# Within a column of weight tiles: long and short matmuls in groups of two, or one after the other

## The chip, the core and the metric

The kernel runs on one core of one Trainium2 chip, as one program launched once. The metric is the device time of that program in microseconds (us); lower is better. Each kernel is timed several times and the median is given. A core has a matmul engine (TensorE, PE in the profile, whose weight loads the profile lists apart as PEld), a vector engine (VectorE, DVE), a scalar engine (ScalarE, ACT), GpSimd (POOL) and SyncE (SP), which here issues the weight transfers.

## The reference, cut to what matters

```python
for l in range(DEPTH):                                   # DEPTH = 2, SEQ = 256, D_MODEL = 2048
    h = _rmsnorm(x, norm1_g[l])
    p = (h @ w_in[l]).astype(f32)                        # 2048 -> 6144
    q, k, v, g, xb, yb = jnp.split(p, ...)
    o_ret = _retention(q, k, v, g, ...)                  # 8 heads
    o_lru = _rg_lru_branch(xb, yb, ...)                  # 1024 channels
    mix = jnp.concatenate([o_ret, o_lru], axis=-1)
    x = x + mix @ w_out[l]                               # 2048 -> 2048
    h = _rmsnorm(x, norm2_g[l])
    x = x + (silu(h @ ffn_w_gate[l]) * (h @ ffn_w_up[l])) @ ffn_w_down[l]   # 2048 -> 5632 -> 2048
return _rmsnorm(x, final_g)
```

Everything is float32. Nearly all of the work is in the matrix products with `w_in`, `w_out`, `ffn_w_gate`, `ffn_w_up` and `ffn_w_down`, for 256 tokens.

## The kernel before

**Float32 in three products.** A float32 number is split in two parts that the matmul engine takes in its one-pass format fp32r: hi is the number rounded to that format, lo is what is left. A product is then hi·hi + hi·lo + lo·hi. For weights, `split` (line 560 on) makes hi with a ScalarE copy (L568) and lo with a VectorE subtraction (L569), in two halves of a unit's weights. For activations, `pair` makes one tile `op` of 2 x 256 columns, hi beside lo.

**A column unit.** The weights of one block of 128 output channels are one unit, up to 16 tiles of 128 x 128. `column_unit` (L182) runs it: for each tile k, a long matmul (L195) with the weights' hi part moves the whole `op` tile, 512 columns, and a short one (L198) with the weights' lo part moves its hi half, 256 columns, into the right half of the same PSUM bank. All matmuls of a unit add into one bank `acc_ps` of 512 columns. When the unit is done the two halves are added by ScalarE and VectorE (L178, L179) or added to the residual (L406, L407). Below, H is a long matmul (L195) and L a short one (L198), each with its own load of 128 x 128 weights, and a pair is the H and the L of one tile.

**The order.** A unit is issued in blocks of four tiles. In each block the kernel takes two tiles at a time (L193): H, H, L, L, then the next two tiles the same way. A unit of 16 tiles is eight such groups; one of 14 tiles seven; one of 15 tiles seven and a last tile alone, H, L.

There are 384 column units in the two layers: 80 of `w_in` (16 tiles), 32 of `w_out` (16), 176 of gate and up (16), 64 of `w_down` with 15 tiles and 32 with 14. That is 80·16 + 32·16 + 176·16 + 64·15 + 32·14 = 6016 tiles. The columns of `w_in` that give v are computed by other code (`v_units`, L441 to L443), where three long matmuls of 512 columns follow one another in turn; the change does not touch them.

**What runs beside it.** The weights of unit n + 2 are split in two halves while unit n runs (at its blocks 0 and 2), and the transfer of unit n + 3 is issued then. There are three buffers each of raw weights, hi and lo, and four PSUM banks for units. A list of ticks places the small work of the heads (scores, decays, normalization) between blocks; their small matmuls, of tile `sm_ps`, stand between blocks on PE. The engines' queues are laid down when the program is built, by a scheduler that may move an instruction past neighbours it does not depend on.

Of the kernel before, what the change touches and what calls it, by code (L numbers as in the profile page):

```python
# [80 lines left out]
def trunk(ctx: ExitStack, tc, a, out):  # L81
# [100 lines left out]
    def column_unit(src, n_k, operand, done, begin=None, order=None):  # L182

        u = Unit(src, n_k * P, [], begin=begin)
        order = order or list(range(n_k))

        def block(i):
            ks = order[i : i + 4]

            def run():  # L190
                if i == 0:
                    u.ps = big_ps.tile([P, 512], F32, tag="big", name="acc_ps")
                for pr in (ks[:2], ks[2:]):  # L193
                    for k in pr:
                        PE.matmul(u.ps, lhsT=u.hi[:, k * P : (k + 1) * P],  # L195
                                  rhs=operand(k).rearrange("p a t -> p (a t)"), start=k == order[0], stop=False)
                    for k in pr:
                        PE.matmul(u.ps[:, T : 2 * T], lhsT=u.lo[:, k * P : (k + 1) * P], rhs=operand(k)[:, 0, :],  # L198
                                  start=False, stop=k == order[-1])
            return run  # L200

        u.blocks += [block(i) for i in range(0, n_k, 4)]
        u.done = lambda: done(u.ps)
        return u
# [542 lines left out]
```

## Time and profile before

| | |
|---|---|
| median of 3 runs | 2257.88 us (2257.45 to 2258.04) |
| the profiled execution | 2257.48 us |
| its span, first to last instruction | 2255.7 us |
| PE busy | 2239.1 us (99%) |
| PEld busy | 1949.4 us (86%) |
| DVE busy | 1512.5 us (67%) |
| ACT busy | 1127.1 us (50%) |
| granted TensorE clock, mean | 0.998 |

The span is the profiled execution without what lies around it, 1.8 us here. Busy time of PE is the union of its matmuls' records; the records overlap, since a matmul's record runs on while the next has begun. How fast the matmuls follow one another is therefore read from their starts, not from their durations. A row of the timeline merges instructions of one line that follow one another, and gives the start of the first.

### The profile page before, as it was taken

The numbers are of one execution on the slowest core, as the hardware profiler recorded it, in microseconds if no ns is written. First come the engines' busy times: TensorE is split into PE (matmuls) and PEld (weight loads), VectorE is DVE, ScalarE is ACT, GpSimd is POOL, SyncE is SP. The second block draws the span as 40 slices with busy tenths as digits, with TensorE's granted clock in tenths as the row PEclk, the third lists the DMA queues.
The fourth block names the chain that finished last, engine by engine and source line by source line (L and its number), as shares of the span: only waits on it lengthen the run. The fifth ranks groups of instructions, "written<-read, shape, count | busy, mean of one in ns | idle before, by whom it ended". The sixth has DMA issues, their size and how long they took to land.

```text
span 2255.7 us, 31764 instructions
## 1 busy us (share of the span) xinstructions
PE 2239.1 (99%) x12760; PEld 1949.4 (86%) x12760; DVE 1512.5 (67%) x2405; ACT 1127.1 (50%) x1648; POOL 59.8 (3%) x97
## 2 busy tenths in 40 slices
PE   9999999999999999999999999999999999999997
PEld 7888888888888888888888888888888888888886
DVE  6888876666566655666748889766665666556665
ACT  6667544544344443444546665444443444334453
POOL 0010100000000000000000101000000000000000
PEclk9999999999999999999999999999999999999999
DMA  7555555555555555555555554555555555555553
GB/s 286 183 186 181 172 195 191 183 191 189 184 200 187 186 186 189 188 190 179 201 193 179 180 197 165 189 182 192 191 183 195 188 187 184 192 188 190 193 175 112
DMA packets 63140, 422.92 MB, mean 187 GB/s; under 512 B 7312, under 2 KB 7952, under 8 KB 24592
## 3 DMA queue, kind: packets, MB, share of 16 engines
q1 hardware_dynamic: 60912, 414.60, 52.5%
q0 software_dynamic: 1792, 5.24, 0.8%
q8 instruction: 100, 1.64, 0.3%
q10 hardware_dynamic: 288, 1.05, 0.1%
q14 instruction: 48, 0.39, 0.0%
HBM read 418.77 MB, written 2.10 MB: 187 GB/s over the span
## 4 chain that ended last, share of the span: by engine, by line
PE 97%; DVE 1%; issue 0%; DMA 0%; POOL 0%; ACT 0%; SPq 0%; DVEq 0%; POOLq 0%
PE acc_ps L195 62%; PE acc_ps L198 31%; PE v_ps L442 1%; PE v_ps L443 1%; PE v_ps L441 1%; PE sm_ps L331 1%; DVE wlo L569 0%; PE sm_ps L240 0%; DMA raw<-in_w_v_dram 0%; DVE op L130 0%; PE sm_ps L289 0%; PE sm_ps L157 0%; PE sm_ps L241 0%; PE sm_ps L256 0%; PE sm_ps L255 0%
## 5 line engine op out<-in xcount | busy, mean ns | idle before, releaser
L195 PE MATMUL acc_ps<-op,whi 128*128 128x512 f32 x6016 | 1899.8, 397 | 0.0
L198 PEld LDWEIGHTS acc_ps<-op,wlo 128*128 128x128 f32 x6016 | 1129.8, 188 | 263.4
L569 DVE TENSOR_TENSOR wlo<-raw,whi 128x1024 fp32r<-128x1024 f32 (+3 forms) x808 | 950.0, 1187 | 366.6 <-ACT whi L568 362.4
L198 PE MATMUL acc_ps<-op,wlo 128*128 128x256 f32 x6016 | 1188.6, 278 | 0.0
L568 ACT ACTIVATE whi<-raw 128x1024 fp32r<-128x1024 f32 (+3 forms) x808 | 817.3, 1029 | 657.3 <-PE acc_ps L195 578.1
L195 PEld LDWEIGHTS acc_ps<-op,whi 128*128 128x128 f32 x6016 | 920.4, 189 | 4.8 <-DVE op L127 0.7
L406 DVE TENSOR_TENSOR x<-acc_ps,x 128x256 f32<-128x256 f32 x128 | 54.2, 424 | 215.5 <-PE acc_ps L198 215.5
L126 ACT ACTIVATE op<-mix 128x256 fp32r<-128x256 f32 x104 | 43.1, 416 | 167.7 <-DVE mix L510 163.5
L505 ACT ACTIVATE sg<-z 128x256 f32<-128x256 f32 x88 | 36.8, 419 | 161.1 <-DVE z L504 161.1
L179 DVE TENSOR_TENSOR z<-acc_ps,low 128x256 f32<-128x256 f32 x256 | 106.7, 417 | 0.0
L178 ACT ACTIVATE low<-acc_ps 128x256 f32<-128x256 f32 x256 | 93.7, 366 | 0.0
L127 DVE TENSOR_TENSOR op<-mix,op 128x256 fp32r<-128x256 f32 x104 | 44.0, 424 | 42.7 <-ACT op L126 42.6
L509 DVE TENSOR_TENSOR sg<-sg,rs 128x256 f32<-128x256 f32 x88 | 37.4, 425 | 42.6 <-ACT sg L505 42.6
L407 DVE TENSOR_TENSOR x<-acc_ps,x 128x256 f32<-128x256 f32 x128 | 54.2, 424 | 4.3
L150 POOL TENSOR_TENSOR rc<-rc,mhalf 128x2 f32<-128x2 f32 x7 | 5.8, 824 | 1720.7 <-DVE rc L149 1720.7
L442 PE MATMUL v_ps<-wlo,op 128*128 128x512 f32 x128 | 50.1, 391 | 1.1 <-DVE wlo L569 1.1
L441 PE MATMUL v_ps<-whi,op 128*128 128x512 f32 x128 | 50.1, 396 | 0.5 <-ACT op L129 0.4
L443 PE MATMUL v_ps<-whi,op 128*128 128x512 f32 x128 | 50.1, 391 | 0.0
L510 DVE TENSOR_TENSOR mix<-z,sg 128x256 f32<-128x256 f32 x88 | 36.7, 417 | 0.0
L504 DVE TENSOR_TENSOR z<-z,rs 128x256 f32<-128x256 f32 x88 | 36.7, 417 | 0.0
L129 ACT ACTIVATE op<-x,par 128x256 fp32r<-128x256 f32 x64 | 31.2, 496 | 2.6 <-DMA par<-in_par_dram 1.8
L173 DVE TENSOR_TENSOR acc<-acc,sq 128x256 f32<-128x256 f32 x73 | 30.6, 420 | 1.6 <-ACT sq L172 1.0
(116 smaller groups left out, 698.9 us busy)
## 6 DMA issues: line engine op xcount, KB each, us to landing
raw<-in_w_gate_dram SPq DMA_DIRECT2D x88, 1024.0 KB, 4.8
raw<-in_w_up_dram SPq DMA_DIRECT2D x88, 1024.0 KB, 4.8
raw<-in_w_in_dram SPq DMA_DIRECT2D x80, 1024.0 KB, 4.8
raw<-in_w_down_dram SPq DMA_DIRECT2D x64, 960.0 KB, 4.7
raw<-in_w_out_dram SPq DMA_DIRECT2D x32, 1024.0 KB, 4.8
raw<-in_w_down_dram SPq DMA_DIRECT2D x32, 896.0 KB, 4.6
raw<-in_w_v_dram SPq DMA_DIRECT2D x12, 1024.0 KB, 4.8
raw<-in_w_v_dram SPq DMA_DIRECT2D x16, 256.0 KB, 6.0
```

The costliest lines, as they stand in the source:

```text
L127: V.tensor_tensor(out=t[:, 1, :], in0=x_ap, in1=t[:, 0, :].bitcast(F32), op=ALU.subtract)
L178: S.activation(out=low, in_=ps[:, T : 2 * T], func=AF.Copy)
L179: V.tensor_tensor(out=z, in0=ps[:, 0:T], in1=low, op=ALU.add)
L195: PE.matmul(u.ps, lhsT=u.hi[:, k * P : (k + 1) * P], rhs=operand(k).rearrange("p a t -> p (a t)"), start=k == order[0], stop=False)
L198: PE.matmul(u.ps[:, T : 2 * T], lhsT=u.lo[:, k * P : (k + 1) * P], rhs=operand(k)[:, 0, :], start=False, stop=k == order[-1])
L406: V.tensor_tensor(out=X[:, k, :], in0=ps[:, T : 2 * T], in1=X[:, k, :], op=ALU.add)
L407: V.tensor_tensor(out=X[:, k, :], in0=ps[:, 0:T], in1=X[:, k, :], op=ALU.add)
L441: PE.matmul(ps, lhsT=x2[:, 0, t], rhs=u.hi[:, w], start=k == 0, stop=False)
L442: PE.matmul(ps, lhsT=x2[:, 0, t], rhs=u.lo[:, w], start=False, stop=False)
L443: PE.matmul(ps, lhsT=x2[:, 1, t], rhs=u.hi[:, w], start=False, stop=k == KD - 1)
L568: S.activation(out=u.hi[:, w], in_=u.raw[:, w], func=AF.Copy)
L569: V.tensor_tensor(out=u.lo[:, w], in0=u.raw[:, w], in1=u.hi[:, w].bitcast(F32), op=ALU.subtract)
```

## The change

One line of `column_unit` changes.

```diff
                 if i == 0:
                     u.ps = big_ps.tile([P, 512], F32, tag="big", name="acc_ps")
-                for pr in (ks[:2], ks[2:]):
+                for pr in (ks[:2], ks[2:3], ks[3:]) if i == 0 else [[k] for k in ks]:
                     for k in pr:
                         PE.matmul(u.ps, lhsT=u.hi[:, k * P : (k + 1) * P],
                                   rhs=operand(k).rearrange("p a t -> p (a t)"), start=k == order[0], stop=False)
```

The first two tiles of a unit keep H, H, L, L. Every other tile is taken alone: its H, then its L. No instruction is added or removed, and the operands of each are the same.

On PE, here are the first matmuls of one `w_in` unit of the first layer (`acc_ps` is its bank, `op` the tile k's activations, `whi` and `wlo` the unit's weights), in the kernel before:

```order
L195 MATMUL acc_ps_2101<-op_142,whi_1956 128x512
L195 MATMUL acc_ps_2101<-op_147,whi_1956 128x512
L198 MATMUL acc_ps_2101<-op_142,wlo_1957 128x256
L198 MATMUL acc_ps_2101<-op_147,wlo_1957 128x256
L195 MATMUL acc_ps_2101<-op_152,whi_1956 128x512
L195 MATMUL acc_ps_2101<-op_162,whi_1956 128x512
L198 MATMUL acc_ps_2101<-op_152,wlo_1957 128x256
L198 MATMUL acc_ps_2101<-op_162,wlo_1957 128x256
L195 MATMUL acc_ps_2101<-op_169,whi_1956 128x512
L195 MATMUL acc_ps_2101<-op_182,whi_1956 128x512
L198 MATMUL acc_ps_2101<-op_169,wlo_1957 128x256
L198 MATMUL acc_ps_2101<-op_182,wlo_1957 128x256
```

and in the changed kernel:

```order
L195 MATMUL acc_ps_2101<-op_142,whi_1956 128x512
L195 MATMUL acc_ps_2101<-op_147,whi_1956 128x512
L198 MATMUL acc_ps_2101<-op_142,wlo_1957 128x256
L198 MATMUL acc_ps_2101<-op_147,wlo_1957 128x256
L195 MATMUL acc_ps_2101<-op_152,whi_1956 128x512
L198 MATMUL acc_ps_2101<-op_152,wlo_1957 128x256
L195 MATMUL acc_ps_2101<-op_162,whi_1956 128x512
L198 MATMUL acc_ps_2101<-op_162,wlo_1957 128x256
L195 MATMUL acc_ps_2101<-op_169,whi_1956 128x512
L198 MATMUL acc_ps_2101<-op_169,wlo_1957 128x256
L195 MATMUL acc_ps_2101<-op_182,whi_1956 128x512
L198 MATMUL acc_ps_2101<-op_182,wlo_1957 128x256
```

From the third tile on, the second H of a group and the first L have changed places. The last L of a group stands where it stood, so a unit begins and ends with the same kinds of matmul.

The scheduler also moves a few neighbours on the other engines. On VectorE, in the last third of `w_down` (14 tiles a unit; L569 makes lo of the weights, L173 and L130 belong to the norm that follows), before:

```order
L406 TENSOR_TENSOR x<-acc_ps,x 128x256
L407 TENSOR_TENSOR x<-acc_ps,x 128x256
L569 TENSOR_TENSOR wlo<-raw,whi 128x896
L173 TENSOR_TENSOR acc<-acc,sq 128x256
L569 TENSOR_TENSOR wlo<-raw,whi 128x896
L130 SCALAR_TENSOR_TENSOR op<-x,par,op 128x256
```

and in the changed kernel:

```order
L406 TENSOR_TENSOR x<-acc_ps,x 128x256
L407 TENSOR_TENSOR x<-acc_ps,x 128x256
L569 TENSOR_TENSOR wlo<-raw,whi 128x896 x2
L173 TENSOR_TENSOR acc<-acc,sq 128x256
L130 SCALAR_TENSOR_TENSOR op<-x,par,op 128x256
```

The second half of the split now stands ahead of the norm's addition. At six other places in the two layers a neighbour on VectorE or ScalarE has moved by one or two instructions in the same way; GpSimd and SyncE are as before.

## Rows read from the trace of the kernel before

**Rows 1.** The page: span, busy time of engines, granted clock, chain that ended last.

```profile
span 2255.7 us, 31764 instructions
...
PE 2239.1 (99%) x12760; PEld 1949.4 (86%) x12760; DVE 1512.5 (67%) x2405; ACT 1127.1 (50%) x1648; POOL 59.8 (3%) x97
...
PEclk9999999999999999999999999999999999999999
...
PE acc_ps L195 62%; PE acc_ps L198 31%; PE v_ps L442 1%; PE v_ps L443 1%; PE v_ps L441 1%; PE sm_ps L331 1%; DVE wlo L569 0%; PE sm_ps L240 0%; DMA raw<-in_w_v_dram 0%; DVE op L130 0%; PE sm_ps L289 0%; PE sm_ps L157 0%; PE sm_ps L241 0%; PE sm_ps L256 0%; PE sm_ps L255 0%
```

**Rows 2.** Waits of PE alone: who, for whom: us in total, times, longest us.

```profile
PE sm_ps L289 <- DVE on L275: 2.1, 2, 1.0
PE sm_ps L666 <- DVE sq L538: 1.4, 1, 1.4
PE v_ps L442 <- DVE wlo L569: 1.1, 2, 0.6
PE sm_ps L614 <- DVE sp L584: 1.0, 1, 1.0
PE sm_ps L157 <- POOL rc L150: 1.0, 1, 1.0
PE v_ps L441 <- ACT op L129: 0.4, 2, 0.2
```

**Rows 3.** Timeline, PE, gate and up units: start us, us, engine, line, op.

```profile
400.81 0.63 PE L195 MATMUL acc_ps<-op,whi 128*128 128x512 f32 x2
401.28 0.39 PE L198 MATMUL acc_ps<-op,wlo 128*128 128x256 f32 x2
401.51 0.62 PE L195 MATMUL acc_ps<-op,whi 128*128 128x512 f32 x2
...
551.29 0.63 PE L195 MATMUL acc_ps<-op,whi 128*128 128x512 f32 x2
```

**Rows 4.** Timeline, PE, units of 14 tiles.

```profile
1057.81 0.63 PE L195 MATMUL acc_ps<-op,whi 128*128 128x512 f32 x2
...
1116.33 0.63 PE L195 MATMUL acc_ps<-op,whi 128*128 128x512 f32 x2
```

**Rows 5.** Timeline, PE, units of 15 tiles: the last tile alone, the next unit.

```profile
577.58 0.40 PE L195 MATMUL acc_ps<-op,whi 128*128 128x512 f32 x1
577.81 0.28 PE L198 MATMUL acc_ps<-op,wlo 128*128 128x256 f32 x1
577.92 0.62 PE L195 MATMUL acc_ps<-op,whi 128*128 128x512 f32 x2
...
578.62 0.63 PE L195 MATMUL acc_ps<-op,whi 128*128 128x512 f32 x2
...
635.48 0.64 PE L195 MATMUL acc_ps<-op,whi 128*128 128x512 f32 x2
635.96 0.40 PE L198 MATMUL acc_ps<-op,wlo 128*128 128x256 f32 x2
636.20 0.62 PE L195 MATMUL acc_ps<-op,whi 128*128 128x512 f32 x2
...
640.73 0.62 PE L195 MATMUL acc_ps<-op,whi 128*128 128x512 f32 x2
```

**Rows 6.** Timeline, PE, units of v: long matmuls only.

```profile
1133.89 0.39 PE L441 MATMUL v_ps<-whi,op 128*128 128x512 f32 x1
1134.12 0.39 PE L442 MATMUL v_ps<-wlo,op 128*128 128x512 f32 x1
...
1170.39 0.39 PE L443 MATMUL v_ps<-whi,op 128*128 128x512 f32 x1
```

**Rows 7.** Timeline, PE and PEld, one group: weight loads beside the matmuls.

```profile
1000.95 0.39 PE L198 MATMUL acc_ps<-op,wlo 128*128 128x256 f32 x2
1000.95 0.19 PEld L198 LDWEIGHTS acc_ps<-op,wlo 128*128 128x128 f32 x1
1001.06 0.30 PEld L195 LDWEIGHTS acc_ps<-op,whi 128*128 128x128 f32 x2
1001.17 0.63 PE L195 MATMUL acc_ps<-op,whi 128*128 128x512 f32 x2
```

**Rows 8.** Timeline, PE and DVE: a unit's start, the split in it, two units later.

```profile
1014.41 0.40 PE L195 MATMUL acc_ps<-op,whi 128*128 128x512 f32 x1
1015.52 1.22 DVE L569 TENSOR_TENSOR wlo<-raw,whi 128x1024 fp32r<-128x1024 f32 x1 [1.64 <-ACT whi L568]
...
1017.00 1.21 DVE L569 TENSOR_TENSOR wlo<-raw,whi 128x1024 fp32r<-128x1024 f32 x1
...
1025.56 0.40 PE L195 MATMUL acc_ps<-op,whi 128*128 128x512 f32 x1
```

## The prediction

> **What bounds the kernel now.** I read the page first: PE is busy 99% of the span, and 93% of the chain that ended last is L195 and L198 [rows 1]. The waits come next: PE waits for another engine some 7 us in all [rows 2], and none of these waits is of a column unit. The granted clock is at nine tenths or more in all 40 slices, with a mean of 0.998, so TensorE stands at the upper of its two levels, 2.4 GHz [rows 1]. The kernel is therefore a stream of matmuls that follow one another at PE's own pace, and the change permutes that stream. Nothing but the pace can answer to it, so the pace is what the rest of the reading is about.
>
> The pace is read from starts. From 400.81 to 551.29 lie 27 gate and up units without a break, 27 x 16 = 432 pairs of H and L: 150.48 / 432 = 348.3 ns a pair, or 696.7 ns a group H, H, L, L [rows 3]. From 1057.81 to 1116.33 lie 12 units of 14 tiles, 168 pairs: 58.52 / 168 = 348.3 ns again [rows 4]. The border between two units thus costs nothing, and the group is all there is to explain. Inside one group the starts read 400.81, 401.28, 401.51: the two H's take 0.47 us and the two L's 0.23 [rows 3].
>
> **The change part by part.** *What moves.* Each unit keeps its first group. Of the 6016 tiles that leaves 6016 - 2 x 384 = 5248, of which 64 (the last of a 15-tile unit) stood alone already. So 5184 tiles, in 2592 groups, go from H, H, L, L to H, L, H, L. No instruction, byte or flop comes or goes. The sum is 5184 times the difference between a pair in the new order and 348.3 ns: each nanosecond is 5.2 us, 0.23% of the kernel. That is the whole difficulty, and 0.2% (4.5 us) is also about what a measurement of this kernel can tell from no change.
>
> *The fixed part of a matmul.* Another stream in the same trace has long matmuls only. The v units run from 1133.89 to 1170.39 in 161 steps, 36.50 / 161 = 226.7 ns a matmul of 512 columns [rows 6]. If 512 columns at 2.4 GHz take 213.3 ns, one by clock, what is left is 13.4 ns a matmul. A group has four matmuls and 2 x 512 + 2 x 256 = 1536 columns: 640.0 + 4 x 13.4 = 693.6 ns. Measured are 696.7, so some 3.1 ns of a group are not explained by the number of matmuls and columns. Order can act on these, and their size is that of the disputed term: 2592 x 3.1 = 8.0 us. A group has one change from long to short and one back, one H after H and one L after L. If the 3.1 ns belong to the changes of length, the new order has them in every pair, and 8.0 us are added. If they belong to the repeats, L after L above all, the new order has none, and 8.0 us go. Neither row decides it by itself; the resolution of the starts (0.01 us over 161 steps, 0.06 ns) is not the problem.
>
> *What a lone pair costs.* The one place where the trace already shows the new order is the last tile of a 15-tile unit: L, L, H, L, H, H [rows 5]. From 577.92 to 640.73 lie 12 such units, 62.81 us; at 348.3 ns a pair the 180 pairs would take 62.70. So each of these units is 0.11 / 12 = 9 ns longer than its number of pairs asks, and since borders are free [rows 4], that is the price of setting one lone H, L into a stream of groups. The pair itself is nearly the usual length, 577.58 to 577.92, 0.34 to 0.35 us. The rest comes behind it: the first group of the next unit takes 0.70 us in one unit (577.92 to 578.62) and 0.72 in another (635.48 to 636.20), and these two kinds alternate [rows 5]. A lone pair is never shown to gain anything, which speaks for the changes of length as what costs, not the repeats. I take +8.0 us for the pairs from this.
>
> *The way back at the head of each unit.* The changed kernel returns to H, H, L, L in every unit's first group, as the 15-tile units do now. Of the 9 ns 1.6 are in the term above (3.1 / 2); 7.4 remain. The 64 units of 15 tiles pay it already: (384 - 64) x 7.4 = 2.4 us. Its bounds are 0 and 9 ns, 0 to 2.9 us.
>
> *Weight loads.* Each matmul has its load, which starts as the matmul ahead of it starts: the load of the second L is at 1000.95, when the first L starts, and that of the next H at 1001.06, 0.11 before 1001.17 [rows 7]. The next load therefore lies beside the current matmul, and a short one leaves about 0.11 us for it. In both orders two loads of each group lie beside a long matmul and two beside a short one, so the count asks for nothing. Whether two tight loads in a row (before) or one tight and one easy in turn (after) is the better is the question of the 3.1 ns again.
>
> The Trainium skill ("TensorE: Matmul & The Clock Gate", sections "Back-to-back issue gap" and "Step-by-step: what each phase is for") says that the next weights are loaded into a background buffer while a matmul streams, and that warm matmuls follow one another at columns / 2.4 + 2.5 ns. An estimate from it is 215.8 + 109.2 = 325.0 ns a pair in either order, so the change would be worth nothing. The trace does not agree on the amount (348.3 ns [rows 3]), so something beside columns and that floor is paid here, and the page does not say whether it asks for an order; that the order is free is the first rival below.
>
> *Waits, buffers and the other engines.* The last H of a unit now ends one L later ahead of the unit's end, about 0.12 us nearer to it, and it frees that unit's hi buffer; the split that takes the buffer is of a later unit. In the unit that starts at 1014.41 the two halves of lo are made at 1015.52 and 1017.00, and PE reads them two units later, from 1025.56 on [rows 8]. The cover is 7 us or more against 0.12 us. In the last third of w_down the second half of the split is moved ahead of the norm's addition on VectorE, which moves each by about one instruction, some 1.2 us at most by the length of a split [rows 8]; VectorE is busy 67% of the span [rows 1] and nothing on PE waits for it there [rows 2]. Without that cover each such delay would be 0.1 to 1.2 us in a unit. I count 0, with 0 to 1 us in all as the range. The small matmuls stand between blocks as before.
>
> The sum: 8.0 + 2.4 = +10.4 us. Against the profiled execution, 2257.48 us (span 2255.7 and 1.8 around it), this gives 2267.9; that execution lies 0.4 below the median of the runs, so the median after should be about 2268.3.
>
> **The rivals.**
>
> *The order is free.* Each matmul costs its columns and a fixed part wherever it stands, and the 3.1 ns are something that any mixture of lengths pays. Then only the way back is left: 2257.9 + 2.4 = 2260.3 us, +0.1%. For it: v's fixed part explains 693.6 of 696.7 ns. Against it: the 9 ns of a lone pair show that the order acts.
>
> *The repeats were the cost* (faster). L after L puts two loads in a row under matmuls that leave 0.11 us each [rows 7]; a long matmul between them gives the loads time again. Its place is the second L of each group, its price at most the 3.1 ns: -8.0 + 2.4 = -5.6 us, 2252.3 us. It decides once the steady pair is below 348.3 - 0.5 ns, where it outweighs the way back. For it: a stream without any repeats of L, v's, has no such remainder. Against it: inserting a pair without repeats costs time in rows 5.
>
> *Every lone pair costs what the last tile of a 15-tile unit costs* (much slower). If the 9 ns are the pair's own, paid each time an H follows a single L, then 5184 x 9 = 46.7 us, 2304.6 us, +2.1%. For it: it is the only direct sight of the new order. Against it: the pair's own starts are 0.34 to 0.35 us apart, and the time is lost in every second following group alone, as on a return to groups.
>
> That the change does not do what it says is hardly possible: the order of PE's instructions shows it, and no engine can make PE idle by as much as is at stake.
>
> **How the numbers follow.** Forecast (changes of length cost): 0.42. Order free: 0.28. Repeats cost: 0.17. Every pair as the lone one: 0.13. The first gives slower by over 0.2%; so does the last; the second is within 0.2%; the third is just faster, and a part of it stays within. A part of the forecast, where half the 3.1 ns act, falls within too. Slower 0.52, same 0.31, faster 0.17. The range reaches from 2251, somewhat below the faster rival, to 2302, short of the full price of the last one; what is left out is a gain of more than the unexplained 3.1 ns and a full 9 ns a pair. The likely part of it is 2258 to 2274.
>
> **What would show it.** In the changed kernel's timeline the start of a gate or up unit and that of one 20 units later give the pace. By the forecast a unit of 16 tiles takes 5573 + 14 x 1.6 + 7 = 5603 ns; free order gives 5573 to 5580, costly repeats about 5558, the last rival 5573 + 126 = 5699. Units of 15 and 14 tiles should go the same way by their number of pairs. PE's waits should stay at some 7 us, the clock at 1.00, and the other engines' busy time where it is. I am wrong if the pair in the middle of a unit is not slower than 348.3 ns, or if a new wait of PE for L568 or L569 appears; and the size is wrong if the loss lies at unit heads only.

## The result, and the profile after

The changed kernel takes 2277.69 us (median of 4 runs, 2276.94 to 2278.06) against 2257.96 us of the kernel before on the same chip: +19.7 us, a ratio of 1.0088 with a 95% interval of 1.0075 to 1.01. It is slower, as forecast, and inside the range of 2251 to 2302 us, but by nearly twice the 10.4 us of the forecast.

The page of the changed kernel, the lines that answer to [rows 1]:

```profile
span 2275.9 us, 31764 instructions
...
PE 2259.0 (99%) x12760; PEld 1960.6 (86%) x12760; DVE 1515.0 (67%) x2405; ACT 1127.3 (50%) x1648; POOL 60.2 (3%) x97
...
PEclk9999999999999999999999999999999999999999
```

The instructions and the clock are the same, and the other engines' busy time nearly so (VectorE 2.5 us more, the loads 11.2); the span is 20.2 us longer and PE is busy 19.9 us longer. PE's waits in the changed kernel, who for whom, us in total, times, longest:

```profile
PE sm_ps L289 <- DVE on L275: 1.8, 2, 1.0
PE sm_ps L666 <- DVE sq L538: 1.4, 1, 1.4
PE v_ps L442 <- DVE wlo L569: 1.2, 2, 0.7
...
PE v_ps L441 <- ACT op L129: 0.9, 1, 0.9
```

With the two rows left out (1.0 us each) these are 7.3 us, against 7.0 in [rows 2]: no new wait. The time is in PE's pace. The timeline of PE in the changed kernel, in the same stretch of gate and up units as [rows 3] (start us, us, engine, line, op):

```profile
414.37 0.62 PE L195 MATMUL acc_ps<-op,whi 128*128 128x512 f32 x2
414.83 0.40 PE L198 MATMUL acc_ps<-op,wlo 128*128 128x256 f32 x2
415.06 0.40 PE L195 MATMUL acc_ps<-op,whi 128*128 128x512 f32 x1
415.30 0.28 PE L198 MATMUL acc_ps<-op,wlo 128*128 128x256 f32 x1
415.41 0.40 PE L195 MATMUL acc_ps<-op,whi 128*128 128x512 f32 x1
...
555.53 0.40 PE L195 MATMUL acc_ps<-op,whi 128*128 128x512 f32 x1
```

From 414.37 to 555.53 lie 25 units: 141.16 / 25 = 5.646 us, where the kernel before takes 5.573. The head of the unit, the group that was kept, takes 0.69 us (414.37 to 415.06), no more than a group did. The 14 pairs behind it take the other 4.95 us, some 353 to 354 ns each instead of 348.3. Over 176 gate and up units that is 176 x 0.073 = 12.9 us, two thirds of the loss. Summed over the trace, `w_in` adds 2.5 us, `w_out` 2.2 and `w_down` 2.2.

The units of 15 tiles show something else (answering to [rows 5]):

```profile
582.39 0.62 PE L195 MATMUL acc_ps<-op,whi 128*128 128x512 f32 x2
...
583.08 0.40 PE L195 MATMUL acc_ps<-op,whi 128*128 128x512 f32 x1
...
583.79 0.40 PE L195 MATMUL acc_ps<-op,whi 128*128 128x512 f32 x1
...
587.67 0.64 PE L195 MATMUL acc_ps<-op,whi 128*128 128x512 f32 x2
...
588.39 0.40 PE L195 MATMUL acc_ps<-op,whi 128*128 128x512 f32 x1
...
589.08 0.40 PE L195 MATMUL acc_ps<-op,whi 128*128 128x512 f32 x1
...
592.90 0.39 PE L195 MATMUL acc_ps<-op,whi 128*128 128x512 f32 x1
```

Two neighbouring units with the same instructions take 5.28 and 5.23 us, and so on in turn. (Units of 14 tiles take turns too, 4.94 and 4.86 us.) In the first, two pairs take 0.71 us (583.08 to 583.79); in the second 0.69 (588.39 to 589.08). Between the recorded starts, which the trace holds in whole nanoseconds, the alternating part of the first repeats every three pairs: H 236, L 113, H 233, L 117, H 241, L 120, together 1060 ns, 353.3 a pair. That of the second repeats every two: H 231, L 113, H 233, L 117, some 693 ns, 346.7 a pair. The second is faster than the groups of the kernel before (348.3). So one order of instructions runs at two paces, called the fast and the slow one below, and that had to be explained before the size could be.

### The profile page after: what moved, and what is told of

Read it like the earlier page. It is cut to its first block, busy times and chain, and to the rows that moved or that the text cites. A ratio compares the mean times of both kernels' runs of the same rounds, so it can differ in the third digit from the quotient of the medians.

```text
span 2275.9 us, 31764 instructions
## 1 busy us (share of the span) xinstructions
PE 2259.0 (99%) x12760; PEld 1960.6 (86%) x12760; DVE 1515.0 (67%) x2405; ACT 1127.3 (50%) x1648; POOL 60.2 (3%) x97
## 4 chain that ended last, share of the span: by engine, by line
PE 97%; DVE 1%; issue 1%; POOL 0%; DMA 0%; ACT 0%; SPq 0%; DVEq 0%; POOLq 0%
PE acc_ps L195 61%; PE acc_ps L198 31%; PE v_ps L442 1%; PE v_ps L443 1%; PE v_ps L441 1%; PE sm_ps L331 1%; DVE wlo L569 0%; PE sm_ps L240 0%; DMA raw<-in_w_v_dram 0%; PE sm_ps L157 0%; DVE op L130 0%; PE sm_ps L289 0%; PE sm_ps L241 0%; PE sm_ps L256 0%; PE sm_ps L255 0%
## 5 line engine op out<-in xcount | busy, mean ns | idle before, releaser
L195 PE MATMUL acc_ps<-op,whi 128*128 128x512 f32 x6016 | 2099.9, 398 | 0.0
L198 PE MATMUL acc_ps<-op,wlo 128*128 128x256 f32 x6016 | 1623.8, 280 | 0.0
L195 PEld LDWEIGHTS acc_ps<-op,whi 128*128 128x128 f32 x6016 | 1105.7, 188 | 240.6 <-DVE op L127 1.3
L569 DVE TENSOR_TENSOR wlo<-raw,whi 128x1024 fp32r<-128x1024 f32 (+3 forms) x808 | 948.8, 1189 | 385.2 <-ACT whi L568 378.1
L173 DVE TENSOR_TENSOR acc<-acc,sq 128x256 f32<-128x256 f32 x73 | 30.6, 419 | 1.0 <-ACT sq L172 1.0
```

What stands on the lines that cost most here:

```text
L195: PE.matmul(u.ps, lhsT=u.hi[:, k * P : (k + 1) * P], rhs=operand(k).rearrange("p a t -> p (a t)"), start=k == order[0], stop=False)
L569: V.tensor_tensor(out=u.lo[:, w], in0=u.raw[:, w], in1=u.hi[:, w].bitcast(F32), op=ALU.subtract)
```

## The experiments

Three theories went in. **Theory 1**, the prediction's: each change between long and short costs, now sized from 353.3 against 348.3 ns. **Theory 2**: strict alternation has a fast and a slow steady pace, and what comes ahead of it decides which. **Theory 3**: reading the same activation tile twice in a row costs. All experiments are edits of the kernel before: the order inside a block is made by a function, and the rest of the kernel is as it was, where nothing else is said.

```diff
-                for pr in (ks[:2], ks[2:]):
-                    for k in pr: ...H of k
-                    for k in pr: ...L of k
+                for what, k in plan(i): ...H or L of k
```

**Alternation throughout.**

```diff
+            return [(w, k) for k in ks for w in "HL"]
```

> Every tile of a unit goes H, L, the first two as well, so no group H, H, L, L is left. Theory 1 (each change between long and short costs; sized anew from the changed kernel, whose gate and up units run at 353.3 ns a pair in their alternating part against 348.3 in groups): 353.3 ns a pair throughout, 5653 ns a unit of 16 tiles, 6016 x 5.0 = +30 us, 2288 us. Theory 2 (strict alternation has two steady paces, 346.7 and 353.3 ns a pair, and the group at a unit's head decides which one a unit falls into): without that group the stream keeps one pace from unit to unit until small matmuls break it, 5547 or 5653 ns a unit in long stretches, and 2248 us if it is the fast one nearly everywhere, 2288 if the slow one. Theory 3 (reading the same activations twice in a row costs): as theory 1, 2288 us.

Measured: 2268.44 us, ratio 1.005 (1.0034 to 1.0065), and the runs lie far apart, 2265.69 to 2274.41, where those of the kernel before lie between 2257.49 and 2258.67. PE's timeline shows both paces (here L200 is H):

```profile
415.23 0.39 PE L200 MATMUL acc_ps<-op,whi 128*128 128x512 f32 x1
...
553.89 0.39 PE L200 MATMUL acc_ps<-op,whi 128*128 128x512 f32 x1
...
655.72 0.40 PE L200 MATMUL acc_ps<-op,whi 128*128 128x512 f32 x1
...
802.71 0.40 PE L200 MATMUL acc_ps<-op,whi 128*128 128x512 f32 x1
...
897.50 0.39 PE L200 MATMUL acc_ps<-op,whi 128*128 128x512 f32 x1
...
1052.81 0.39 PE L200 MATMUL acc_ps<-op,whi 128*128 128x512 f32 x1
...
2020.55 0.40 PE L200 MATMUL acc_ps<-op,whi 128*128 128x512 f32 x1
...
2178.84 0.40 PE L200 MATMUL acc_ps<-op,whi 128*128 128x512 f32 x1
```

The first two rows are 25 gate and up units apart, 400 pairs: 138.66 / 400 = 346.7 ns. The next two are 26 such units of the next third of the same layer, 416 pairs: 146.99 / 416 = 353.3 ns. Same code, same shapes, same granted clock (1.00 in both stretches). Each stretch keeps its pace for some 140 us and more. A new pace is taken where PE is interrupted: in the first unit of 15 tiles, for one, the H behind one L starts after 289 ns instead of 112 to 118. The last four rows are the 28 units of the last third in the first and in the second layer, 448 pairs each: 155.31 / 448 = 346.7 ns in the one and 158.29 / 448 = 353.3 in the other. So even the same units, with the same work beside them (VectorE is busy 95.90 us in both stretches), can fall out either way. This is theory 2. It would also explain why the runs differ, but that is not shown, since only the slowest of the four was traced. A cost per change of length (theory 1) or per repeated tile (theory 3) gives one pace and is not enough.

**Groups of four.**

```diff
+            return [(w, k) for w in "HL" for k in ks]
```

> Groups of four: H, H, H, H, L, L, L, L, half as many changes of length as in the kernel before. Theory 1: 343.3 + 2.5 = 345.8 ns a pair, -15 us, 2243 us. Theory 2: nothing below the fast pace of 346.7 ns, and grouped orders keep some 348.3: 2248 to 2258 us. Theory 3: no tile is read twice in a row before or now, so 2258 us.

Measured: 2270.38 us, ratio 1.0053 (1.0036 to 1.007). All three expectations miss. Its timeline (L200 is H, L203 is L):

```profile
414.70 1.09 PE L200 MATMUL acc_ps<-op,whi 128*128 128x512 f32 x4
415.63 0.64 PE L203 MATMUL acc_ps<-op,wlo 128*128 128x256 f32 x4
...
555.03 0.40 PE L200 MATMUL acc_ps<-op,whi 128*128 128x512 f32 x1
```

25 units, 140.33 / 400 = 350.8 ns a pair: half the changes of length, and slower than twos. A fixed price per change falls with this.

**The short matmul one tile late.**

```diff
+            res = []
+            for j, k in enumerate(ks, i):
+                res.append(("H", k))
+                if j: res.append(("L", order[j - 1]))
+            return res + [("L", order[-1])] * (i + 4 >= n_k)
```

> Alternation with the short matmul one tile late: H0, H1, L0, H2, L1, ..., H15, L14, L15. Long and short still alternate as in the changed kernel, but no two neighbours read the same activation tile. Theory 1: as the changed kernel, 353.3 ns a pair within a unit, about 2277 us. Theory 2: again one of the two paces, 346.7 or 353.3 ns, decided by the two H's at the head and two L's at the end: 2250 to 2280 us. Theory 3: the cost is gone, at most 348.3 ns a pair, 2258 us or less.

Measured: 2281.21 us, ratio 1.0102 (1.0087 to 1.0117). From 415.14 to 556.48 lie 25 units: 141.34 / 400 = 353.3 ns.

```profile
415.14 0.40 PE L205 MATMUL acc_ps<-op,whi 128*128 128x512 f32 x1
...
556.48 0.40 PE L205 MATMUL acc_ps<-op,whi 128*128 128x512 f32 x1
```

No two neighbours share an activation tile here, and the loss is all there. Theory 3 is out from this side.

**H, L, L, H.**

```diff
+            res = []
+            for pr in (ks[:2], ks[2:]):
+                for j, k in enumerate(pr):
+                    res += [("H", k), ("L", k)] if j == 0 else [("L", k), ("H", k)]
+            return res
```

> H0, L0, L1, H1, H2, L2, L3, H3: lengths come in twos as in the kernel before, but at each change of length the two neighbours read the same activation tile. Theory 1: same number of changes, 348.3 ns a pair, 2258 us. Theory 2: a stream of twos has one pace, 348.3 ns, 2258 us. Theory 3: as many repeated tiles as in the changed kernel, so about 353 ns a pair, 2278 us or more.

Measured: 2258.24 us against 2258.11, ratio 1.0 (0.9991 to 1.001). In its gate and up units these two rows lie 25 units apart (L204 is H):

```profile
412.42 0.40 PE L204 MATMUL acc_ps<-op,whi 128*128 128x512 f32 x1
...
551.75 0.40 PE L204 MATMUL acc_ps<-op,whi 128*128 128x512 f32 x1
```

139.33 / 400 = 348.3 ns a pair. Tiles are shared at every change and nothing is lost, so theory 3 is out from the other side as well. What counts is the sequence of lengths.

**No short matmuls, in twos and in turn.** The L of both kernels moves all 512 columns, which adds the product lo·lo.

```diff
-                        PE.matmul(u.ps[:, T : 2 * T], lhsT=..., rhs=operand(k)[:, 0, :], ...)
+                        PE.matmul(u.ps[:, 0:512], lhsT=..., rhs=operand(k).rearrange("p a t -> p (a t)")[:, 0:512], ...)
```

> The order of the kernel before, but the matmul with the weights' lo part moves all 512 columns, as the other does (the product lo x lo is added, so all 6016 short matmuls become long). It measures the fixed part of a matmul alone, without short ones. If the paces come from weight loads that a short matmul leaves too little time for: every matmul 226.7 ns as in v, 453.3 ns a pair, 2258 + 6016 x 0.105 = about 2890 us. If they come from the order of weight tiles or of hi and lo: more than 453.3, by some 1 to 5 ns a pair, 2896 to 2920 us.

> As the run with 512 columns in twos, but in turn H, L, H, L throughout. If a short matmul is what makes the order matter: 453.3 ns a pair again, in every unit and at one pace, about 2890 us, the same as in twos within 0.1%. If alternation as such costs: about 5 ns a pair more than in twos, +30 us, or two paces side by side in its units.

Measured: 2888.24 and 2888.00 us. The gate and up units start, 25 units apart, at 513.09 and 694.42 us in twos and at 513.14 and 694.48 in turn:

```profile
513.09 0.39 PE L200 MATMUL acc_ps<-op,whi 128*128 128x512 f32 x1
...
694.42 0.39 PE L200 MATMUL acc_ps<-op,whi 128*128 128x512 f32 x1
```

```profile
513.14 0.39 PE L200 MATMUL acc_ps<-op,whi 128*128 128x512 f32 x1
...
694.48 0.39 PE L200 MATMUL acc_ps<-op,whi 128*128 128x512 f32 x1
```

Both are 453.3 ns a pair, 226.7 a matmul, as in v [rows 6]. With equal lengths the order of hi and lo is free and there is one pace. The order matters only because lengths differ.

**A short matmul of 384 columns, in turn.** Against the run before this one:

```diff
-                        PE.matmul(u.ps[:, 0:512], lhsT=...
+                        PE.matmul(u.ps[:, 0:384], lhsT=...
-                                  rhs=operand(k).rearrange("p a t -> p (a t)")[:, 0:512], ...)
+                                  rhs=operand(k).rearrange("p a t -> p (a t)")[:, 0:384], ...)
```

> H, L in turn throughout, the short matmul with 384 columns instead of 256. The sum of columns and fixed parts (213.3 + 160.0 + 2 x 13.3) is 400.0 ns a pair, about 2569 us. If a short matmul is too short for a weight load only near 256 columns: 400.0 ns everywhere, one pace. If any mixture of lengths has two paces: 400 in some units and about 407 in others, up to 2610 us.

Measured: 2636.15 us, more than either expectation. PE's timeline, first w_out units, then gate and up units (L200 is H, L203 is L):

```profile
363.33 0.39 PE L200 MATMUL acc_ps<-op,whi 128*128 128x512 f32 x1
...
434.91 0.39 PE L200 MATMUL acc_ps<-op,whi 128*128 128x512 f32 x1
...
468.75 0.40 PE L200 MATMUL acc_ps<-op,whi 128*128 128x512 f32 x1
468.99 0.34 PE L203 MATMUL acc_ps<-op,wlo 128*128 128x384 f32 x1
469.17 0.40 PE L200 MATMUL acc_ps<-op,whi 128*128 128x512 f32 x1
...
634.09 0.40 PE L200 MATMUL acc_ps<-op,whi 128*128 128x512 f32 x1
```

11 units take 71.58 us, 406.7 ns a pair; 25 others 165.34 us, 413.4 ns a pair. The sum of columns and fixed parts is 400.0: 6.7 and 13.4 ns are lost, again at two paces. A 384-column matmul leaves its load 0.18 us (468.99 to 469.17), against 0.11 with 256 columns [rows 7], and the loss is greater, not smaller. That a short matmul is too short for the next load, the mechanism of the second rival, is therefore not what costs. A load's record still lasts longer (0.19 us [rows 7]) than the 0.18, but the groups of eight below point the same way: there an L in a run of L's keeps to 120 ns.

**Steering.** If theory 2 holds, the pace can be chosen. The rule in the expectation was read from the starts in the changed kernel alone.

```diff
+            twos = {16: 8, 15: 4, 14: 12}[n_k]
+            prs = (ks[:2], ks[2:]) if i < twos else [[k] for k in ks]
```

> Orders chosen to steer into the fast pace. Read from the changed kernel: alternation falls into the fast pace (346.7 ns) after a group H, H, L, L that ends 116, 112 ns and into the slow one (353.3) after one that ends 113, 119; groups in a row are of these two kinds in turn; after a fast stretch the first group is of the slow kind, after a slow stretch it depends on the number of its pairs modulo 3. So an even number of groups keeps a fast stretch fast, and a count of pairs that is 2 modulo 3 turns a slow one: 4 groups and 8 pairs in a unit of 16, 2 and 11 in one of 15, 6 and 2 in one of 14. Theory 2: gate and up units 8 x 348.3 + 8 x 346.7 = 5560 ns, 15-tile units 5207, in all -5.6 us, 2252 us. Theory 1 (alternation costs 5 ns a pair wherever it stands): 3072 pairs, +15 us, 2273 us. If the paces can't be steered: some units at 5560 and others at 5613, between 2252 and 2270 us.

Measured: 2255.89 us against 2258.00, ratio 0.999 (0.9981 to 0.9999). The paces are as expected: the gate and up units 25 apart start at 412.86 and 551.86, 139.00 / 25 = 5.560 us.

```profile
412.86 0.40 PE L202 MATMUL acc_ps<-op,whi 128*128 128x512 f32 x1
...
551.86 0.40 PE L202 MATMUL acc_ps<-op,whi 128*128 128x512 f32 x1
```

3072 pairs alternate in this kernel, more than half of what the change moves, and it is not slower than the kernel before but 2.1 us faster; theory 1 had it 15 us slower. The gain is less than 5.6 us. The trace tells where half of the missing 3.5 us went: from the first unit of w_in to the first of w_out it takes 244.90 us in the first layer and 244.81 in the second, against 244.52 and 244.47 in the kernel before, where the fast pace would have saved 0.5 in each. Units of w_in that small matmuls interrupt take longer than in groups (5706 ns instead of 5661, for one); undisturbed ones take the 5560 that were expected.

**The short matmul in the left half of the bank, in twos and in turn.** The halves are added in the end, so the short product may go to either.

```diff
-                        PE.matmul(u.ps[:, T : 2 * T], lhsT=...
+                        PE.matmul(u.ps[:, 0:T], lhsT=...
```

> The order of the kernel before; the short matmul adds into the left half of the PSUM bank (columns 0 to 255) instead of the right half, which the sum of the two halves allows. If the paces come from how soon a column of PSUM is added to again (right half: an L follows its H's column by 256 columns, an H follows L's by 512; left half: the other way round), the pace of 348.3 ns a pair changes. If only the sequence of lengths counts: 348.3 ns, 2258 us.

> H, L in turn throughout, with the short matmul in the left half of the bank. PSUM theory: one pace, or paces other than 346.7 and 353.3 ns. Sequence of lengths alone: 346.7 in some stretches and 353.3 in others, as with the right half, 2265 to 2275 us.

Measured: 2258.27 us (ratio 1.0, 0.999 to 1.001) and 2269.54 us (1.005, 1.0031 to 1.0068). In twos 25 units lie between 411.72 and 551.05, 348.3 ns a pair. In turn, both paces are there again:

```profile
415.51 0.39 PE L200 MATMUL acc_ps<-op,whi 128*128 128x512 f32 x1
...
554.18 0.39 PE L200 MATMUL acc_ps<-op,whi 128*128 128x512 f32 x1
...
650.35 0.40 PE L200 MATMUL acc_ps<-op,whi 128*128 128x512 f32 x1
...
808.64 0.40 PE L200 MATMUL acc_ps<-op,whi 128*128 128x512 f32 x1
```

138.67 / 400 = 346.7 ns in the first 25 units, 158.29 / 448 = 353.3 in the last 28. How soon a column of the bank is added to again does not matter.

**Steering the feed-forward part alone.** w_in and w_out stay in twos; every third gate or up unit opens with two groups.

```diff
+            prs = (ks[:2], ks[2:]) if i < twos else [[k] for k in ks]        # twos=16 unless given
-                res.append(column_unit(a["w_gate"][l, f], KD, lambda k: st["h2", k], gate))
+                res.append(column_unit(a["w_gate"][l, f], KD, lambda k: st["h2", k], gate, twos=4 * (2 * f % 3 == 0)))
-                res.append(column_unit(a["w_up"][l, f], KD, lambda k: st["h2", k], up))
+                res.append(column_unit(a["w_up"][l, f], KD, lambda k: st["h2", k], up, twos=4 * ((2 * f + 1) % 3 == 0)))
-                res.append(column_unit(a[f"w_down{t}"][l, n], nf, ..., done))
+                res.append(column_unit(a[f"w_down{t}"][l, n], nf, ..., done, twos=4 if nf == 15 else 12))
```

> Steering where no small matmuls interfere: w_in and w_out stay in twos; of the gate and up units every third one begins with two groups, all its other tiles and the two units behind it alternate (2 groups and 44 pairs, 44 = 2 modulo 3); w_down as in the steered kernel. Theory 2: a fast stretch stays fast, 5547 to 5550 ns a gate or up unit instead of 5573, 5207 instead of 5233 for 15 tiles: 176 x 25 + 64 x 26 = 6.1 us less if all are fast, about 5 us with some units lost at the start of each third, 2253 us. Theory 1: 2275 us.

Measured: 2253.58 us against 2258.14, ratio 0.998 (0.9971 to 0.9989), 4.6 us less: the fastest kernel of this study, better than both. Its timeline, gate and up units, then units of 15 tiles:

```profile
412.33 0.40 PE L201 MATMUL acc_ps<-op,whi 128*128 128x512 f32 x1
...
545.51 0.40 PE L201 MATMUL acc_ps<-op,whi 128*128 128x512 f32 x1
...
577.80 0.39 PE L201 MATMUL acc_ps<-op,whi 128*128 128x512 f32 x1
...
629.87 0.39 PE L201 MATMUL acc_ps<-op,whi 128*128 128x512 f32 x1
```

24 gate and up units: 133.18 / 384 = 346.8 ns a pair. Ten units of 15 tiles: 52.07 / 10 = 5.207 us, where the kernel before takes 5.234 [rows 5]. w_in takes what it takes in the kernel before (244.50 us in the first layer). Nearly the order that the change makes, H and L in turn, is here faster than the groups; in these units all that differs from the changed kernel is where groups stand between the pairs.

**Groups of eight.**

```diff
+            res = [("H", k) for k in ks]
+            return res + [("L", k) for k in order[i - 4 : i + 4]] * (i % 8 == 4)
```

> Groups of eight H and eight L. Theory 1 (fewer changes are better): below 345.8 ns a pair, under 2243 us; the run in fours already speaks against it. If long runs of one length are what costs (348.3 in twos, 350.8 in fours): above 350.8, over 2270 us. If the cost of a group is a fixed one: 10 ns a group of four found in fours, spread over eight tiles, about 349 ns, 2262 us.

Measured: 2264.89 us, ratio 1.003 (1.0018 to 1.0042); the third expectation is the nearest. Its timeline (L201 is H, L204 is L):

```profile
413.57 2.00 PE L201 MATMUL acc_ps<-op,whi 128*128 128x512 f32 x8
415.41 1.11 PE L204 MATMUL acc_ps<-op,wlo 128*128 128x256 f32 x8
416.36 2.00 PE L201 MATMUL acc_ps<-op,whi 128*128 128x512 f32 x8
...
553.23 0.40 PE L201 MATMUL acc_ps<-op,whi 128*128 128x512 f32 x1
```

25 units: 139.66 / 400 = 349.2 ns a pair. Inside a group eight H's take 1.84 us and eight L's 0.95 (415.41 to 416.36). Eight H's of 226.7 would be 1.81. The trace's starts, in ns from each matmul to the next, read H 233, 236, 228, 233, 231, 226, 227, 227, then L 113 and 119 and six times 120. So a change of length is felt over several matmuls behind it: the first five H's take some 28 ns too long in all, the first two L's 8 too few. An L in a run of L's comes to rest at 120 ns, which is 256 columns at 2.4 GHz, 106.7, and the same 13.3 ns of fixed part as in v. So the floor of a pair is 226.7 + 120.0 = 346.7 ns, the fast pace exactly, and every order can be written as this floor and a price of its changes of length:

| order | ns a pair | above 346.7, ns a group (one run of H's and one of L's) |
|---|---|---|
| in turn, fast pace | 346.7 | 0 |
| in turn, slow pace | 353.3 | 6.7 |
| twos | 348.3 | 3.3 |
| fours | 350.8 | 16.7 |
| eights | 349.2 | 20 |

The price of going from H to L and back is 20 ns where the runs are long, and less where the next change comes before the stream has settled; what it comes to in ones depends on the state in which the stream enters. That the price is cut short by the next change is a reading of this table and of the starts in eights, not tested by itself.

## Why the prediction came out as it did

- **What bounds the kernel.** Right: the loss is PE's pace; the clock stands as before, there is no new wait, and the other engines' busy time hardly moves.
- **The count.** Right: 5184 tiles moved. The loss is 19.7 us / 5184 = 3.8 ns for each, a mean over units at 353.3 and units at 346.7.
- **The fixed part, 13.4 ns, and 3.1 ns of a group left over.** Right, and the best step: 13.3 ns is the fixed part wherever a run of equal lengths lets it be read, at 512 columns (226.7) and at 256 (120.0), and what is left over comes with changes of length, as the prediction chose. The 512-column runs show it: no change of length, no remainder, no effect of order. But changes need not cost: the fast pace has one at every matmul and no remainder.
- **+8.0 us for the pairs.** Right in sign, mis-sized, and this is the step that did not hold. It took a price per change that is the same everywhere, 1.6 ns a pair. Measured are +5.0 ns in the slow pace and -1.6 in the fast one. In the gate and up units, which are in the slow pace nearly throughout, the term is 176 x 14 x 5.0 = 12.3 us alone. The sign is in part luck: nothing in the prediction says that these units would stay in the slow pace, and in the fast one the same term is a gain. In units of 15 tiles even the size comes out, 5233 + 13 x 1.6 = 5254 ns, but as the mean of 5283 and 5224 in turn.
- **The 9 ns of a lone pair.** The rows held the answer and it was averaged away. The prediction noted that the group behind a lone pair took 0.70 and 0.72 us in turn, and called the mean a price. Two values in turn from the same instructions are two states, and the right question was in which one the new order would stay.
- **+2.4 us for the way back at the head of each unit.** Wrong as a cost in the gate and up units: the head group takes 0.69 us there, and 0.72 only in the units of 15 tiles that turn fast (587.67 to 588.39). Its effect is to set the pace of the pairs behind it. With 14 alternating pairs behind each head nearly all units are slow; with 13 or 12 they take turns. That the slow pattern of three pairs comes back to the same state after 14 is a reading of the starts. The two steered kernels chose their counts by such a rule and got the paces it asks for where no small matmuls stand between.
- **Loads, buffers, split.** Counted at nothing, and no wait on them shows that they cost anything.
- **The rivals.** "The order is free" falls with five different paces for the same matmuls. "The repeats were the cost" had the right size for the fast pace, 346.7 ns, but not its cause: with 384 columns there is more room for loads and more loss, and the slow pace has no repeats either. What spoke for it, that v has no such remainder, could not count, since the fixed part was taken from v. "Every lone pair costs 9 ns" asked too much: 5.0 in the slow pace, and a gain in the fast one.

Open is what in TensorE holds the state. The runs exclude the tile that is read, the half of the bank that is written, the waits and the clock, and speak against the room for the load; they leave the sequence of lengths, the fixed part of a matmul, and a memory that reaches over several matmuls.

## What to carry to other kernels

Where matmuls of different lengths follow one another without a gap, measure the pace over some hundred of them, and write it as columns by the granted clock and a fixed part for each matmul; what is left over may belong to the order, and some of it can be gained, here 4.6 us. Look at the single intervals before a mean is taken: values that alternate between units with the same instructions can be states, as here, and a small change of order then decides between them for whole stretches. Such an order should be tried on the chip in several runs: the runs of the stream that alternates throughout lay 8.7 us apart, and its trace has the same units at either pace.

## What was not expected of the hardware

A stream that only alternates long and short matmuls has two steady paces, 346.7 and 353.3 ns a pair with 512 and 256 columns, 406.7 and 413.4 with 512 and 384. With 256 columns the slow one repeats over three pairs. Each is kept over more than 400 pairs without any difference in what the engines are given. A matmul's fixed part is 13.3 ns here at 256 and at 512 columns. Fewer changes of length are not better by themselves: fours (350.8 ns) and eights (349.2) are slower than twos (348.3).
